# Rotation with copied halves, and other places for the tiles, in a hybrid attention block

## The chip, the cores and the metric

The kernel runs on one core of one Trainium2 chip. The metric is the time on the device of one run, in microseconds (us), as the median of several runs. A core has five engines with queues of their own: TensorE (PE; its weight loads are listed as PEld), VectorE (DVE), ScalarE (ACT), GpSimd (POOL) and SyncE (SP, which starts DMAs).

## What is computed

One decoder block for 512 tokens and width 2048. Its input is normalised and projected, two groups of heads attend in different ways, each head's output is gated by SiLU of a projection, and an output matrix and a second norm follow.

```
h = rmsnorm(x); proj = h @ w_in
qa, kca, vca, ksa, vsa, kwa, vwa, za, ga, qb, kb, vb, zb = split(proj)
qa, kca, ksa, kwa = rope(...)              # first group: 8 heads of 128, 2 key heads
kc, vc = compress(kca), compress(vca)      # blocks of 32 tokens, stride 16, small MLP
o_a = g0 * compressed_attention + g1 * selected_attention + g2 * window_attention
y_a = o_a * silu(za)
o_b = banded_attention(rope(qb), rope(kb), vb, window 128, sinks); y_b = o_b * silu(zb)
out = rmsnorm(x + concat(y_a, y_b) @ w_out)

def rope(x):  x1, x2 = halves(x); return concat(x1*cos - x2*sin, x2*cos + x1*sin)
```

## The kernel before

Every product of large matrices is made in fp32r words: an operand is kept as a high word (ACT rounds it into fp32r) and a low word (DVE subtracts the high word from the operand), and `mm3` (L118 to L121) issues three matmuls, high times high (L119), high times low (L120) and low times high (L121). So each weight tile that arrives in a `raw` buffer is split once by ACT into `whi` and once by DVE into `wlo`.

The stages, in the order of time: statistics and the first projections; from about 77 us the second head group (`softmax_b`, `attn_b`) with its projections, 512 columns wide; from 302 us the value projections (`tok_chunk`) and the compression (`compress_unit`); from 366 us the keys of the first group (`keys`, which calls `seven`, a product of 7 instead of 8 quarter products, as Strassen and Winograd do); from 423 us the eight heads of the first group (`pair`, which also calls `seven`, and `attn_a`); from 631 us the last head together with the first quarter of the output matrix; from 676 us the other quarters by the same seven products; from 789 us the end of the norm and the stores.

The order on each engine is not the order of the code: a scheduler with a model of its own for the time places the instructions, and `issue_after` pins a few.

**The rotation.** Channels lie on partitions, so the two halves of a head are partitions 0 to 63 and 64 to 127. `turn` (L658 to L666) makes two DVE products of 64 partitions, which read one half and the sine and write the other half of `t2` (L661), a product with the cosine (L662), and the sum (L664, on DVE for the keys and the last two heads, on POOL for the others). It runs four times for the keys and once for each head, twelve times in all. `turned` (L805 to L807) does the same for the keys to be compressed, from PSUM, twice, with `rope_mul` (L129 to L133). In `seven` the rotation of a finished row starts in the function `done`, behind the sum for the product "w"; the product "q" and the next row's products follow.

**Places.** Tiles lie at fixed addresses in each partition. In `words` (L82 and L83) the word tiles are 1088 elements wide and a unit of 1024 starts 0, 16, 32 or 48 elements in (MOVING, EVEN, STILL, BELOW), so that its start differs by 64 bytes. Small tiles named `space` move what is allocated behind them. `step` (L125 to L127) is one matmul into an unused bank, with a moving operand that starts at a chosen place.

## Time and profile before

| | us |
|---|---|
| median of 3 runs | 802.01 (801.76, 802.01 and 909.72) |
| the profiled execution | 802.8, of which its span is 801.0 |
| PE busy in the span | 789.6 |
| DVE busy | 686.3 |
| ACT busy | 504.7 |

Times in the rows are us from the start of the span, and a mean is in ns. Matmuls overlap in the pipeline: the listed length of one reaches from its start to its modelled end, and is longer than the step from one start to the next. TensorE's clock is granted in full (1.00, 2.4 GHz) in the stages from 302 to 789 us.

### The profile page before, as it was taken

To read this page: it belongs to the slowest core of one execution; us is meant where nothing else is said; L and a number is where in the kernel's file an instruction comes from. 1 tells how busy PE (TensorE), PEld (TensorE's weight loads), DVE (VectorE), ACT (ScalarE), POOL (GpSimd) and SP (SyncE) were. 2 spreads that over 40 slices of the span, in tenths; PEclk is the share of its full clock that TensorE was granted. 3 is DMA by queue.
4 is the path that set the end of the run, shared out by engine and by line. 5 is a ranking of instruction groups with operands and counts; after the bars stand their busy time and mean duration, and the time that the engine had idled before them with its cause. 6 is when DMAs were issued, how large, how long until landed. Compare 5 with 4: busy or idle time off the path is not lost.

```text
span 801.0 us, 15316 instructions
## 1 busy us (share of the span) xinstructions
PE 789.6 (99%) x5693; PEld 739.1 (92%) x5693; DVE 686.3 (86%) x1407; ACT 504.7 (63%) x1103; POOL 108.3 (14%) x111
## 2 busy tenths in 40 slices
PE   9999999999999999999999999999999999999996
PEld 8788888888888899999999999999999999999996
DVE  7668988889989597759999999998999798978895
ACT  6646657655666356664447778777777867553545
POOL 3615002110121000323210110110100000000000
PEclk9999999999999999999999999999999999999998
DMA  7572243564373469887723213225216836797845
GB/s 239 172 242 81 79 144 106 171 171 150 101 210 106 158 200 281 257 269 194 207 82 106 68 53 119 82 92 159 71 50 216 296 120 219 257 266 193 258 86 211
DMA packets 49563, 131.05 MB, mean 164 GB/s; under 512 B 6000, under 2 KB 8848, under 8 KB 49488
## 3 DMA queue, kind: packets, MB, share of 16 engines
q1 hardware_dynamic: 43376, 110.89, 42.3%
q0 software_dynamic: 5824, 18.65, 10.5%
q8 instruction: 45, 0.74, 0.4%
q10 hardware_dynamic: 288, 0.52, 0.2%
q14 instruction: 30, 0.25, 0.1%
HBM read 113.23 MB, written 16.81 MB: 162 GB/s over the span
## 4 chain that ended last, share of the span: by engine, by line
PE 86%; DVE 6%; DMA 3%; ACT 2%; issue 2%; POOL 0%; SPq 0%; DVEq 0%; ACTq 0%
PE pj L119 16%; PE pj L121 15%; PE pj L120 15%; PE oa L120 5%; PE oa L119 5%; PE oa L121 5%; PE sp L932 4%; PE bank L121 2%; PE bank L120 2%; PE bank L119 2%; DMA xr<-xT 2%; DVE wlo L543 2%; PE tp L969 2%; PE tp L384 2%; DMA raw<-wq 1%
## 5 line engine op out<-in xcount | busy, mean ns | idle before, releaser
L119 PE MATMUL pj<-xh,whi 128*128 128x256 f32 (+1 forms) x592 | 196.9, 333 | 0.6 <-ACT t L608 0.5
L121 PE MATMUL pj<-xh,wlo 128*128 128x256 f32 (+1 forms) x592 | 196.2, 331 | 0.0
L120 PE MATMUL pj<-xl,whi 128*128 128x256 f32 (+1 forms) x592 | 196.1, 331 | 0.0
L119 PEld LDWEIGHTS pj<-xh,whi 128*128 128x128 f32 x592 | 111.4, 188 | 11.0 <-ACT t L608 0.9
L121 PEld LDWEIGHTS pj<-xh,wlo 128*128 128x128 f32 x592 | 111.4, 188 | 10.1
L120 PEld LDWEIGHTS pj<-xl,whi 128*128 128x128 f32 x592 | 111.4, 188 | 9.7
L543 DVE TENSOR_TENSOR wlo<-raw,whi 128x1024 fp32r<-128x1024 f32 (+2 forms) x80 | 92.9, 1172 | 7.8 <-ACT whi L542 7.2
L542 ACT ACTIVATE whi<-raw 128x1024 fp32r<-128x1024 f32 (+2 forms) x80 | 77.6, 985 | 30.7 <-DVE raw L581 11.5
L99 DVE TENSOR_TENSOR wlo<-raw,whi 128x1024 fp32r<-128x1024 f32 (+1 forms) x61 | 72.1, 1184 | 22.8 <-ACT whi L97 22.3
L97 ACT ACTIVATE whi<-raw 128x1024 fp32r<-128x1024 f32 (+1 forms) x60 | 56.6, 945 | 28.8 <-PE pj L120 14.8
L120 PE MATMUL oa<-wlo,xh 128*128 128x256 f32 x200 | 55.5, 278 | 0.0
L119 PE MATMUL oa<-whi,xh 128*128 128x256 f32 x200 | 55.4, 278 | 0.0
L121 PE MATMUL oa<-whi,xl 128*128 128x256 f32 x200 | 55.2, 276 | 0.0
L121 PE MATMUL pj<-pu,wlo 128*128 128x256 f32 x160 | 45.0, 281 | 0.5 <-DVE wlo L543 0.5
L119 PE MATMUL pj<-pu,whi 128*128 128x256 f32 x160 | 45.1, 282 | 0.4 <-DVE zr L581 0.4
L120 PE MATMUL pj<-pu,whi 128*128 128x256 f32 x160 | 44.7, 279 | 0.0
L289 DVE TENSOR_TENSOR pl<-tp,ph 128x512 fp32r<-128x512 f32 (+1 forms) x64 | 40.7, 651 | 3.1 <-ACT ph L288 2.9
L288 ACT ACTIVATE ph<-tp 128x512 fp32r<-128x512 f32 (+1 forms) x64 | 34.1, 560 | 9.6 <-PE tp L969 4.4
L363 ACT ACTIVATE ttb<-ttb,sums 128x256 f32<-128x256 f32 (+1 forms) x64 | 30.0, 471 | 14.4 <-DVE sums L356 14.4
L121 PEld LDWEIGHTS oa<-whi,xl 128*128 128x128 f32 x200 | 37.6, 188 | 0.0
L120 PEld LDWEIGHTS oa<-wlo,xh 128*128 128x128 f32 x200 | 37.6, 188 | 0.0
L119 PEld LDWEIGHTS oa<-whi,xh 128*128 128x128 f32 x200 | 37.5, 188 | 0.0
(401 smaller groups left out, 2369.8 us busy)
## 6 DMA issues: line engine op xcount, KB each, us to landing
raw<-wq SPq DMA_DIRECT2D x41, 512.0 KB, 4.4
raw<-wz SPq DMA_DIRECT2D x36, 512.0 KB, 4.0
cw<-cw SPq DMA_DIRECT2D x32, 256.0 KB, 4.0
raw<-wos SPq DMA_DIRECT2D x14, 512.0 KB, 5.9
rw<-wos SPq DMA_DIRECT2D x10, 512.0 KB, 4.8
xr<-xT SPq DMA_DIRECT2D x16, 256.0 KB, 3.4
rows<-xT SPq DMA_DIRECT2D x8, 512.0 KB, 4.7
raw<-wo SPq DMA_DIRECT2D x8, 512.0 KB, 6.0
```

Of the source, the lines that this page charges most:

```text
L97: last["hi"] = act.activation(hi[:, :width], rw[:, :width], AF.Copy).ins
L99: last["lo"] = dve.tensor_tensor(out=lo[:, :width], in0=rw[:, :width], in1=hi[:, :width].bitcast(F32), op=ALU.subtract).ins
L119: pe.matmul(ps, ah, bh, start=first, stop=False, skip_group_check=go_on)
L120: pe.matmul(ps, ah, bl, start=False, stop=False, skip_group_check=go_on)
L121: recent["mm"] = pe.matmul(ps, al, bh, start=False, stop=last, skip_group_check=go_on).ins
L288: act.activation(ph, tp, AF.Copy)
L289: dve.tensor_tensor(out=pl, in0=tp, in1=ph.bitcast(F32), op=ALU.subtract)
L363: act.activation(tv, tv, AF.Exp, bias=mn[:, e, v:v + 1], scale=-1.0, accum_out=dn[:, e, v:v + 1])
L384: pe.transpose(tp[:, o:o + P], tts[kt + s][:, v, c0:c0 + P], ident)
L542: split_hi = act.activation(hi, src, AF.Copy).ins
L543: last["lo"] = dve.tensor_tensor(out=lo, in0=src, in1=hi.bitcast(F32), op=ALU.subtract).ins
L932: pe.matmul(sp[:, a:b], qq[:, qs], kk[:, ko:ko + b - a], start=pi == 0, stop=pi == 2)
```

## The change

**The rotation.** A new function, `swapped`, has ACT copy each half of the source onto the other half of `t2` (two copies of 64 partitions), and DVE multiply `t2` by the sine in place, all 128 partitions at once. The sine table is loaded with its halves exchanged, by two DMAs. `turn` and `turned` call it. Per rotation two DVE instructions become one, and ACT gets two.

**The places.** `gt` becomes the first tile and 64 bytes long (its last column goes to `small`, by a DMA of its own), `small`, `sums` and others grow or are moved, `vbf` shares the place of `ob`, `xh` and `xl` become two parts of one tile of 64 more elements, the constants for `words` change in six calls, and the low and high words of y are read back 16 elements further on. Nothing is computed in another way. What comes of it at the matmuls is this; the numbers are the start of the moving and of the stationary operand, in bytes within 256, as the two built programs have them:

| matmuls | before: moving, stationary | after |
|---|---|---|
| projections, 512 wide (L119 to L121) | 192, 192 | 192, 192 |
| second group: scores (L349, L350) | 192, 0 | 192, 0 |
| second group: transposes; output (L389, L390) | 128, 192 | 192, 0 |
| `tok_chunk` | 128, 192 | 128, 192 |
| `compress_unit` (L708, L709) | 64, 128 | 128, 192 |
| `seven`: all products | 192, 0 | 192, 0 |
| first group: scores (L932) | 192 or 64, 0 | 192 or 64, 0 |
| first group: transposes; output (L975 to L977) | 128, 192 | 192, 0 |
| output matrix, all quarters | 128, 192 | 192, 0 |

```diff
-MOVING, EVEN, STILL, BELOW = 0, 16, 32, 48
+MOVING, EVEN, STILL = 0, 16, 32
...
-    small = const.tile([P, 8], F32, name="small")
+    small = const.tile([P, 16], F32, name="small")
...
-    gt = const.tile([P, KT + 1], F32, name="gt")
-    rowvalid = gt[:, KT:KT + 1]
+    rowvalid = small[:, 8:9]
...
-    xh = xpool.tile([P, KT, S], F32R, name="xh")
-    xl = xpool.tile([P, KT, S], F32R, name="xl")
+    slabs = xpool.tile([P, 2 * KT * S + 64], F32R, name="x")
+    xh, xl = [slabs[:, e * KT * S:(e + 1) * KT * S].rearrange("p (k s) -> p k s", s=S) for e in range(2)]
...
-            nc.sync.dma_start(sinA, rope[:, 1, :])
+            for a, b in ((0, 64), (64, 0)):
+                nc.sync.dma_start(sinA[a:a + 64], rope[b:b + 64, 1, :])
...
+    def swapped(t2, v):
+        for a, b in ((0, 64), (64, 0)):
+            act.activation(t2[a:a + 64], v[b:b + 64], AF.Copy)
+        dve.tensor_tensor(out=t2, in0=t2, in1=sinA, op=ALU.mult)
+
     def turn(v, out=None, engine=None):
         t2 = wk.tile([P, S], F32, name="t2", tag="t2", bufs=1)
-        for a, b in ((0, 64), (64, 0)):
-            dve.tensor_tensor(out=t2[a:a + 64], in0=v[b:b + 64], in1=sinA[b:b + 64], op=ALU.mult)
+        swapped(t2, v)
         dve.tensor_tensor(out=v, in0=v, in1=cosA, op=ALU.mult)
...
-        t1, t2 = rope_mul(*[wk.tile([P, S], F32, name="t", tag=tag, bufs=1) for tag in tags], ps, cosA, sinA)
+        t1, t2 = [wk.tile([P, S], F32, name="t", tag=tag, bufs=1) for tag in tags]
+        swapped(t2, ps)
+        dve.tensor_tensor(out=t1, in0=ps, in1=cosA, op=ALU.mult)
...
-    places = [words(MOVING), words(BELOW), words(BELOW)]
+    places = [words(MOVING) for n in range(3)]
...
-    yh, yl = [[w[:, (2 * f + 1) % 17, :] for f in range(16)] for w in (xh, xl)]
+    yh, yl = [[slabs[:, (e * KT + (2 * f + 1) % 17) * S + 16:][:, 0:S] for f in range(16)] for e in range(2)]
...
-    step(banks1[3], flat[:, 3 * S - 16:3 * S + 112], flat[:, 2 * S + 32:2 * S + 288])
+    step(banks1[3], flat[:, 2 * S:2 * S + P], flat[:, 3 * S - 16:3 * S + 240])
...
-        hi, lo = to or words(MOVING)
+        hi, lo = to or words(EVEN)
```

The order on DVE at the keys of one head, the last stretch of `keys(1)`. `pj` is the bank of the product, `t` and `zr` the two rows to be rotated, and line numbers are those of each kernel. First the kernel before:

```order
L581 TENSOR_TENSOR t_3958<-t_3958,pj 128x256
L661 TENSOR_TENSOR t_4196<-t_3958,sinA 64x512 x2
L543 TENSOR_TENSOR wlo<-raw,whi 128x1024
L662 TENSOR_TENSOR t_3958<-t_3958,cosA 128x512
L581 TENSOR_TENSOR zr<-zr,pj 128x256
L543 TENSOR_TENSOR wlo<-raw,whi 128x1024
L664 TENSOR_TENSOR t_3958<-t_3958,t_4196 128x512
L661 TENSOR_TENSOR t_4293<-zr,sinA 64x512 x2
```

And DVE at the same place with the change:

```order
L584 TENSOR_TENSOR t_3962<-t_3962,pj 128x256
L546 TENSOR_TENSOR wlo<-raw,whi 128x1024
L664 TENSOR_TENSOR t_4200<-t_4200,sinA 128x512
L669 TENSOR_TENSOR t_3962<-t_3962,cosA 128x512
L584 TENSOR_TENSOR zr<-zr,pj 128x256
L671 TENSOR_TENSOR t_3962<-t_3962,t_4200 128x512
L546 TENSOR_TENSOR wlo<-raw,whi 128x1024
L773 TENSOR_TENSOR k_4207<-t_3962,k_4206 128x512
```

The sine product has moved behind one split of words (`wlo`) and is one instruction instead of two; the sum for `zr`, which frees a bank of PSUM, has four instructions between it and the sum for `t` in the first listing and three in the second.

ACT at that place, before (`whi` is the high word of a unit, `k` the rotated key):

```order
L753 ACTIVATE VC_2840<-vc 128x128
L542 ACTIVATE whi<-raw 128x1024 x2
L608 ACTIVATE t_4248<-pj 128x256
L542 ACTIVATE whi<-raw_4264 128x1024
L765 ACTIVATE k_4201<-t_3958 128x512
```

and with the change:

```order
L760 ACTIVATE VC_2841<-vc 128x128
L545 ACTIVATE whi<-raw 128x1024
L663 ACTIVATE t_4200<-t_3962 64x512 x2
L545 ACTIVATE whi<-raw 128x1024
L772 ACTIVATE k_4206<-t_3962 128x512
L663 ACTIVATE t_4299<-zr 64x512 x2
L611 ACTIVATE t_4254<-pj 128x256
```

The two copies stand between the two splits, so the second split now waits for the row `t_3962` and for the copies.

## Rows read from the trace of the kernel before

**Rows 1.** The page, part 1: busy us, share, instructions per engine.
```profile
PE 789.6 (99%) x5693; PEld 739.1 (92%) x5693; DVE 686.3 (86%) x1407; ACT 504.7 (63%) x1103; POOL 108.3 (14%) x111
```

**Rows 2.** Windows by stage: us, then busy us (instructions) per engine, clock, DMA.
```profile
302.00:366.00 64.00, 63.88 (x529) 63.66 (x528) 44.91 (x105) 39.31 (x96) 16.88 (x24) 1.00 0.87 260
366.00:423.00 57.00, 55.56 (x473) 54.60 (x474) 54.87 (x74) 27.65 (x40) 9.36 (x10) 1.00 0.54 152
423.00:631.00 208.00, 207.79 (x1746) 205.50 (x1746) 193.03 (x429) 160.55 (x401) 16.30 (x10) 1.00 0.36 117
631.00:676.00 45.00, 45.00 (x390) 44.73 (x389) 40.16 (x98) 34.88 (x84) 0.00 (x0) 1.00 0.53 183
676.00:789.00 113.00, 113.00 (x997) 112.86 (x997) 98.97 (x126) 58.18 (x84) 8.55 (x10) 1.00 0.72 205
```

**Rows 3.** Lines by shape, PE, 676 to 789 us: count, busy us, mean ns.
```profile
L120 PE MATMUL oa<-wlo,xh 128*128 128x256 f32 x144 | 39.7, 276 | 0.0
```

**Rows 4.** Windows of 5 us, PE alone: matmuls seen in each.
```profile
366.20:371.20 5.00, 5.00 (x44) 1.00 0.50 142
690.00:695.00 5.00, 5.00 (x46) 1.00 0.47 143
```

**Rows 5.** Lines by shape, PE, 423 to 631 us.
```profile
L120 PE MATMUL pj<-xl,whi 128*128 128x256 f32 x213 | 59.9, 281 | 0.0
...
L120 PE MATMUL pj<-pu,whi 128*128 128x256 f32 x104 | 29.1, 280 | 0.0
...
L120 PE MATMUL pj<-qw,whi 128*128 128x256 f32 x56 | 16.0, 285 | 0.0
...
L975 PE MATMUL op<-ph,VH 128*128 128x256 f32 x54 | 15.2, 282 | 0.0
```

**Rows 6.** Lines by shape, PE, 631 to 676 us.
```profile
L120 PE MATMUL oa<-wlo,xh 128*128 128x256 f32 x56 | 15.8, 282 | 0.0
...
L120 PE MATMUL pj<-wlo,xh 128*128 128x256 f32 x43 | 11.9, 278 | 0.0
```

**Rows 7.** Lines by shape, PE, 302 to 366 us.
```profile
L120 PE MATMUL bank<-wlo,xh 128*128 128x256 f32 x37 | 10.4, 281 | 0.0
...
L708 PE MATMUL bank<-whi,F 128*128 128x256 f32 x32 | 8.1, 280 | 0.0
```

**Rows 8.** Timeline, PE, around four transposes: start us, us, instruction.
```profile
450.59 0.36 PE L119 MATMUL pj<-xh,whi 128*128 128x256 f32 x1
450.79 0.28 PE L120 MATMUL pj<-xl,whi 128*128 128x256 f32 x1
```

**Rows 9.** Lines by shape, DVE, 366 to 423 us.
```profile
L543 DVE TENSOR_TENSOR wlo<-raw,whi 128x1024 fp32r<-128x1024 f32 x18 | 22.7, 1281 | 1.7 <-ACT whi L542 1.6
...
L661 DVE TENSOR_TENSOR t<-t,sinA 64x512 f32<-64x512 f32 x6 | 4.1, 686 | 0.1
...
L661 DVE TENSOR_TENSOR t<-zr,sinA 64x512 f32<-64x512 f32 x4 | 2.7, 686 | 0.1
...
L662 DVE TENSOR_TENSOR t<-t,cosA 128x512 f32<-128x512 f32 x3 | 2.1, 686 | 0.0
```

**Rows 10.** Waits of PE, 366 to 423 us: total us, times, longest us.
```profile
PE pj L121 <- DVE wlo L543: 0.5, 2, 0.3
PE pj L119 <- ACT t L608: 0.5, 1, 0.5
PE pj L119 <- DVE zr L581: 0.4, 1, 0.4
```

**Rows 11.** Timeline, DVE, the first rotation in this form: start us, us.
```profile
374.14 0.42 DVE L581 TENSOR_TENSOR t<-t,pj 128x256 f32<-128x256 f32 x1
...
374.60 1.39 DVE L661 TENSOR_TENSOR t<-t,sinA 64x512 f32<-64x512 f32 x2
...
377.76 0.41 DVE L581 TENSOR_TENSOR zr<-zr,pj 128x256 f32<-128x256 f32 x1
```

**Rows 12.** Chain of waits, 366 to 423 us, shares by line.
```profile
by line: DVE wlo L543 22.1%; DMA raw<-wq 13.1%; issue 12.1%; PE pj L119 10.7%; PE pj L121 10.7%; PE pj L120 10.0%; ACT whi L542 5.6%; DVE raw L581 4.0%; DVE t L661 3.8%; DVE t L581 3.2%; DVE zr L677 3.0%; DVE t L662 2.4%; DVE zr L581 2.3%; 
```

**Rows 13.** Lines by shape, ACT, whole span: a copy that changes partitions.
```profile
L395 ACT ACTIVATE ob<-opb 64x512 f32<-64x512 f32 x16 | 9.5, 594 | 14.0 <-PE opb L390 7.8 <-DVE ob L396 6.0
```

More of the change, by code (lines that the diff above doesn't have):

```diff
@@ L43, in hybrid_block @@
     const = ctx.enter_context(sb("const"))
+    gt = const.tile([P, KT], F32, name="gt")
     wp = ctx.enter_context(sb("wp", bufs=3))
@@ L121, in mm3 @@
         recent["mm"] = pe.matmul(ps, al, bh, start=False, stop=last, skip_group_check=go_on).ins
-    flat = xh.rearrange("p k s -> p (k s)")
+    flat = slabs[:, 0:KT * S]
     def step(bank, still, moving):
@@ L146, in load_x @@
         if k == 0:
-            nc.sync.dma_start(gt, gT)
+            nc.sync.dma_start(gt, gT[:, 0:KT])
         nc.sync.dma_start(xr, xT[:, k, :])
@@ L202, in hybrid_block @@
         nc.sync.dma_start(tab, tabs)
+        nc.sync.dma_start(rowvalid, gT[:, KT:KT + 1])
     dve.tensor_tensor(out=cosB, in0=cosB, in1=rstdb, op=ALU.mult)
@@ L290, in split_pt @@
         return ph, pl
-    vbf = wb.tile([P, NQ, P], F32, name="vbf")
+    vbf = wb.tile([P, NQ, P], F32, name="vbf", tag="ob")
+    KBH = wb.tile([P, 2, S], F32R, name="KBH")
+    KBL = wb.tile([P, 2, S], F32R, name="KBL")
     sk = wb.tile([P, 5, 16], F32, name="sk")
@@ L295, in hybrid_block @@
     act.activation(sk[:, 1, :], sk[:, 0, :], AF.Copy, scale=-1.0)
-    KBH = wb.tile([P, 2, S], F32R, name="KBH")
-    KBL = wb.tile([P, 2, S], F32R, name="KBL")
     VB = wb.tile([P, NQ, 2, P], F32R, name="VB")
@@ L338, in softmax_b @@
         for part in range(2):
-            sums = wk.tile([P, 3, 2, 2], F32, name="sums", tag="sums")
+            sums = wk.tile([P, 6, 2, 2], F32, name="sums", tag="sums")
             mn, dn, ex = sums[:, 0], sums[:, 1], sums[:, 2]
@@ L497, in hybrid_block @@
     VC = [kv.tile([P, P], F32R, name=f"VC{g}") for g in range(2)]
+    kv.tile([P, 48], F32, name="space")
     ahead = ExitStack()
@@ L855, in hybrid_block @@
             cacc[1] = bank(4)
-        compress_unit(1, u, cacc[1], words(BELOW))
+        compress_unit(1, u, cacc[1], words(MOVING))
         if 1 <= u <= 3:
@@ L887, in hybrid_block @@
     KH, KL = [kv.tile([P, CMP + 1056], F32R, name=f"K{e}")[:, 0:CMP + 1024] for e in "HL"]
+    kv.tile([P, 16], F32, name="space")
     for e, k in enumerate((KH, KL)):
@@ L915, in attn_a @@
             tt = wa.tile([P, 1792 if pair else 768], F32, name=f"tt{pair}", tag=f"tt{pair}")
-            sums = wk.tile([P, 2, 2, 3], F32, name="sums", tag="sums")
+            sums = wk.tile([P, 4, 2, 3], F32, name="sums", tag="sums")
             mn, dn = sums[:, 0], sums[:, 1]
@@ L1152, in hybrid_block @@
                      (1, 3, (7,))):
-        hi, lo = load_unit(wo0[:, c, u], 1024, place=MOVING, loaded=first_units.pop(0) if first_units else None, after=last["qh"],
+        hi, lo = load_unit(wo0[:, c, u], 1024, place=EVEN, loaded=first_units.pop(0) if first_units else None, after=last["qh"],
                            after_lo=low_y[11] if (c, u) == (0, 2) else last["turn"])
@@ L1166, in hybrid_block @@
                 combos(m)
+    cmb.tile([P, 48], F32, name="space3")
     banks1 = banks(1)
-    step(banks1[3], flat[:, 3 * S - 16:3 * S + 112], flat[:, 2 * S + 32:2 * S + 288])
+    step(banks1[3], flat[:, 2 * S:2 * S + P], flat[:, 3 * S - 16:3 * S + 240])
     for T in range(2):
@@ L1336, in pair @@
             def pair():
-                return words(MOVING)
+                return words(EVEN)
             def hi(d, src):
```

## Prediction

> **What bounds the kernel now.** I read the page's first part, then the windows by stage, then lines, waits and the chain stage by stage. The first part shows TensorE (PE) busy for 789.6 of 801.0 us and VectorE (DVE) for 686.3 [rows 1]. So what does not shorten PE's own work or its waits changes nothing. The windows then show two kinds of stage [rows 2]. In the heads (423 to 631 us) PE is busy 207.79 of 208.00 us, and at the output matrix (676 to 789) all the time: here only a matmul's own pace counts. At the keys (366 to 423) DVE is busy 54.87 of 57.00 us and PE issues only 473 matmuls, while at the output matrix 997 take 113.00 us, 113.3 ns each. By that pace the keys need 473 x 113.3 ns = 53.6 us of PE. The other 3.4 us of the stage are waits and slower matmuls, and the chain of waits says on whom: the splits into low words on DVE hold 22.1%, the sine products (L661) 3.8% more [rows 12].
>
> The second thing to see is that equal matmuls have two paces. A 128x256 product lists 276 ns at the output matrix [rows 3] and 280 to 285 ns in the heads [rows 5], without a wait ahead of either. That it is a real difference and not one of the listing shows in two windows of 5 us: 46 matmuls against 44 [rows 4], at the same clock (1.00). The change can act on both: the rotation on DVE's load, the places on the pace.
>
> **The change, part by part.**
>
> *Rotation, on DVE.* Twelve calls of `turn` and two of `turned` each lose two products of 64 partitions and get one of 128. A product with 64 partitions costs 686 ns and one with 128 also 686 [rows 9], so each rotation saves DVE 0.69 us, 9.6 us in all. Only those at the keys can matter: ten of the L661 instructions (6 + 4) lie there, five rotations, so DVE's 54.87 us fall by 5 x 0.69 = 3.4 to 51.4 us, under PE's 53.6. How much of it PE gets: its three waits at this stage for DVE or ACT add up to 0.5 + 0.5 + 0.4 = 1.4 us [rows 10]. One can be followed in the order shown: the sum for `zr`, which frees the bank for which PE waits 0.4 us, starts 3.62 us after the sum for `t` (377.76 less 374.14) [rows 11], and with one sine product less in between it starts about 0.69 us earlier. Below, the gain is bounded by nothing (13.1% of the chain there is loads of `wq`, which stay [rows 12]), above by the 3.4 us. I take 1.7: the waits, and a little of the pace that is lost behind them, nearer to the waits since these are seen.
>
> *Rotation, on ACT.* 28 copies are added. The nearest row is a copy of 64 partitions by 512 from PSUM to others, 594 ns [rows 13]; the copies in `turned` are of this kind, those in `turn` read SBUF, so this row is an estimate for them. At the keys ACT gets 10 x 0.594 = 5.9 us on 27.65 of 57; in the heads seven rotations add 14 x 0.594 = 8.3 us on 160.55 of 208 [rows 2]. Both have room, and I cost them at nothing. What hides them at the keys is the split of 1.28 us (L543) [rows 9] that now stands on DVE between the sum and the sine product: two copies take 1.19. Without that cover a rotation is longer than before by 2 x 0.594 + 0.686 - 2 x 0.686 = 0.50 us, and behind the copies wait the next high word and, for it, DVE's low word and PE's product.
>
> *The sine table and `rowvalid`.* Two DMAs instead of one, and one small one more on SP's queue behind the tables at the end of the first stage. Their first readers are far behind them; nothing.
>
> *Places, first group's heads.* Before, products (moving start 192, stationary 0) alternate with transposes and outputs (128, 192); afterwards all are (192, 0), but for parts of the scores. The nearest rows of a stretch where products, transposes and outputs agree are those of the last head with the first quarter of the output matrix, all (128, 192). Count what each stretch has over 276 ns, with the middle line (L120) of each triplet standing for its three. Heads: 3 x (213 x 5 + 104 x 4 + 56 x 9 + 54 x 6) ns = 6.9 us over 1281 matmuls, 5.4 ns each [rows 5]. Last head: 3 x (56 x 6 + 43 x 2) ns = 1.3 us over 297, 4.3 ns each [rows 6]. If the heads come to the same, they gain 1.1 ns x 1281 = 1.4 us, which I take. Bounds: at most 6.9, less what stays because the first product behind transposes is long (360 ns against 280 for the next) [rows 8]; and a loss, if moving starts that jump by 64 bytes were what brings the fast pace back, since then the change takes such jumps away. At worst all 1281 run at 5 ns over, with the long ones on top, about 1 us more than now.
>
> *Places, values and compression (302 to 366 us).* `tok_chunk` and `compress_unit` alternate between (128, 192) and (64, 128), and both become (128, 192). The products list 281 ns and the compression's 280 [rows 7]. At 276 they would gain 3 x 37 x 5 ns and 2 x 32 x 4 ns, 0.8 us together. I take half, 0.4, and nothing as the lower end.
>
> *Places, output matrix.* From (128, 192) to (192, 0), in itself uniform before and after, and at 276 ns before [rows 3]. I take no change.
>
> *A rule against it.* The row shows 46 against 44 matmuls in equal times [rows 4], on stretches whose operands lie at different places but also follow different work. The Trainium skill, "TensorE: Matmul & The Clock Gate", Part 2 (Step-by-step), says that PE has two independent SBUF read ports and that loading the next weights takes no read bandwidth from the running matmul. By that rule a place could not set the pace, and the sum would be the rotation's 1.7 us alone. No row here separates the place from what ran just before, so the rule stands as the first rival.
>
> **Sum.** 1.7 (keys) + 1.4 (heads) + 0.4 (values) = 3.5 us from the profiled execution's 802.8 us (span 801.0 and 1.8 around it): 799.3. That execution is 0.8 us over the median of the runs, 802.0, from which the same sum gives 798.5. I forecast 799.0.
>
> **Rivals.**
>
> 1. *The places do nothing.* The pace comes from the work before, whatever the starts. For it: within one stretch of equal places the lines still read 276 to 285. Only the rotation is left: 802.8 - 1.7 = 801.1 us.
> 2. *The fast pace everywhere.* For it: uniform places go together with 276 ns for 997 matmuls [rows 2, 3]. Against it: the scores still change places, and in the last head uniform places did not suffice [rows 6]. Keys 3.4, values 0.8, and of the heads' 6.9 some 5.5, since the long first products stay: 802.8 - 9.7 = 793.1 us.
> 3. *The output matrix falls into the slow pace.* (192, 0) there is new, and the one `step` that sets it is new too. If those 997 matmuls run 5 ns longer (281 against 276), that is 5.0 us; with the keys' gain and none in the heads 802.8 + 5.0 - 1.7 = 806.1 us, slower. It decides as soon as over 35% of that stage is slow, for then it takes back the 1.7. Against it: a uniform stretch has held the fast pace for 113 us.
> 4. *The copies become the wait.* ACT works in order, and ACT's own waits in front of a copy hold the splits behind it. At 0.50 us for each of the five rotations at the keys that is 2.5 us of PE, with no gain there: 802.8 + 2.5 - 1.8 (heads, values) = 803.5 us. It decides where ACT comes to the copies later than DVE is through its split. ACT's 27.65 busy us of 57 speak against it.
>
> **How the numbers follow.** Forecast (796 to 801, its own range) 0.45; rival 1 (801 to 802) 0.19; rival 2 0.11; rival 3 0.11; rival 4 0.11; something else, beyond 2% either way, 0.03. A range from 793.0 to 805.0 leaves out rival 3, that rest, and about half of rival 2's spread, just under 2 in 10. A change of 2%, 16 us, is about what a measurement of this kernel can tell from no change. None of the cases reaches it: all bounds together are 3.4 + 6.9 + 0.8 = 11.1 us of gain. So faster 0.01, within 2% 0.97, slower 0.02.
>
> **What would show it.** Right: DVE's busy time between the values and the heads falls by about 3.4 us and that stage shrinks by 1 to 2 us; PE's wait for `zr` is gone; outputs of the heads (`op`) list under 282 ns; 997 matmuls of the output matrix still in 113 us. Wrong: DVE's sine product shows idle time in front of it that ends with ACT's copy (rival 4); the lines of the output matrix list 281 (rival 3); the heads' lines are as before and only the stage of the keys is shorter (rival 1). What would break the whole forecast is the scheduler's new interleaving in the heads: a PE that waits there (0.21 us of idle now) would cost more than any term of this sum.

## The result: 0.9% slower, lost in the heads

The changed kernel takes **810.8 us** (809.1 to 811.6 in four runs) against 802.7 of the kernel before beside it: a ratio of **1.0093, 95% interval 1.0076 to 1.0111**. (The ratio is of the fast runs alone, while the median 802.7 still counts a run of 909.7 us, so it is not the quotient of the two medians.) The forecast was 799.0 us with a range to 805.0; it missed, on the slow side. The class of within 2% is right, the sign is not. The profiled execution of the changed kernel took 810.6 us, of which its span is 808.7.

The page's first part, busy us by engine (for the kernel before: [rows 1]):

```profile
PE 794.2 (98%) x5693; PEld 741.5 (92%) x5693; DVE 681.5 (84%) x1393; ACT 523.7 (65%) x1131; POOL 109.1 (13%) x111
```

DVE is busy 4.8 us less, half of the 9.6 that the prediction worked out, and ACT 19.0 us more. The span is 7.7 us longer, of which PE is busy for 4.6.

To compare stage by stage, the borders have to follow the products: a stage goes from its first product to the first one of the next. In the kernel before these are at 291.1 (values, compression and keys), 420.6 (heads), 620.6 (last head with most of the first quarter of the output matrix) and 664.0 (the end of that quarter and, from 678.8, the other three; "output matrix" below). The windows of [rows 2] have the values 11, the heads 2 and the last head 10 us later than this; no term of the sum hangs on it. Windows by stage, the kernel before: us, then busy us (instructions) of PE, its weight loads, DVE, ACT and POOL, clock, DMA.

```profile
291.10:420.60 129.50, 128.46 (x1082) 127.51 (x1081) 107.96 (x204) 71.93 (x149) 26.24 (x34) 1.00 0.73 215
420.60:620.50 199.90, 199.17 (x1668) 196.64 (x1667) 189.25 (x410) 154.39 (x384) 16.30 (x10) 1.00 0.32 101
620.50:664.00 43.50, 43.50 (x376) 43.23 (x374) 36.17 (x90) 31.27 (x73) 0.00 (x0) 1.00 0.56 200
664.00:793.20 129.20, 129.20 (x1140) 129.06 (x1139) 111.12 (x160) 72.52 (x120) 8.55 (x10) 1.00 0.73 218
```

The same four stages of the changed kernel:

```profile
290.80:421.20 130.40, 128.90 (x1084) 127.70 (x1083) 105.32 (x206) 79.07 (x161) 27.49 (x34) 1.00 0.72 215
421.20:626.20 205.00, 202.15 (x1677) 197.74 (x1676) 186.58 (x402) 164.92 (x400) 15.21 (x10) 1.00 0.30 96
626.20:669.60 43.40, 42.65 (x360) 42.06 (x359) 36.43 (x90) 30.47 (x71) 0.00 (x0) 1.00 0.61 216
669.60:801.00 131.40, 131.36 (x1148) 131.17 (x1146) 112.28 (x162) 72.38 (x120) 8.55 (x10) 1.00 0.72 214
```

Of the 7.8 us between the two profiled executions the heads hold 5.0, the output matrix 2.1 and values and keys 1.0. Eight transposes of the last head stand in the heads now, so about 0.9 us of the 5.0 is work that has only moved. In the heads PE now idles 2.85 us where it idled 0.7. What it waits for there (changed kernel, PE, 421 to 626 us; total us, times, longest):

```profile
PE pj L121 <- DVE wlo L546: 0.9, 3, 0.6
PE op L986 <- DVE pl L290: 0.8, 2, 0.7
PE sp L942 <- DVE sums L948: 0.5, 1, 0.5
PE sp L942 <- POOL ql L262: 0.3, 1, 0.3
PE pj L119 <- ACT t L611: 0.3, 1, 0.3
```

There is no single culprit: low words, the low words of the probabilities (`pl`), the low word of the queries (`ql`). What stands behind them is on DVE's list of waits in the same stretch:

```profile
DVE wlo L546 <- ACT whi L545: 5.2, 11, 0.9
...
DVE t L664 <- ACT t L663: 1.4, 4, 0.5
```

DVE, the busy engine of that stage, stands 11 times for ACT's high words and 4 times for ACT's copies (L663). In the kernel before it stands twice for high words there:

```profile
DVE wlo L543 <- ACT whi L542: 0.5, 2, 0.3
```

**One rotation followed.** The row is `t`; its last sum, the sine product, the cosine product, the sum on POOL, the high word `qh` (ACT) and the low word `ql` (POOL) follow each other. The kernel before, timeline of DVE around the second head (start us, us):

```profile
437.38 0.42 DVE L581 TENSOR_TENSOR t<-t,pj 128x256 f32<-128x256 f32 x1
437.83 1.39 DVE L661 TENSOR_TENSOR t<-t,sinA 64x512 f32<-64x512 f32 x2
...
440.39 0.69 DVE L662 TENSOR_TENSOR t<-t,cosA 128x512 f32<-128x512 f32 x1
```

its ACT, with the high word:

```profile
442.58 0.64 ACT L260 ACTIVATE qh<-t 128x512 fp32r<-128x512 f32 x1 [0.94 <-POOL t L664]
```

and its POOL:

```profile
441.24 1.30 POOL L664 TENSOR_TENSOR t<-t,t 128x512 f32<-128x512 f32 x1 [21.12 <-DVE sums L950]
443.29 2.31 POOL L261 TENSOR_TENSOR ql<-t,qh 128x512 fp32r<-128x512 f32 x1 [0.75 <-ACT qh L260]
```

The row is ready at 437.80, the sum starts 3.4 us later, `qh` ends 5.4 us behind the row, and `ql` ends at 445.60. The changed kernel at the same place, DVE:

```profile
437.78 0.42 DVE L584 TENSOR_TENSOR t<-t,pj 128x256 f32<-128x256 f32 x1
...
441.24 0.69 DVE L664 TENSOR_TENSOR t<-t,sinA 128x512 f32<-128x512 f32 x1 [0.37 <-ACT t L663]
441.85 0.69 DVE L669 TENSOR_TENSOR t<-t,cosA 128x512 f32<-128x512 f32 x1
```

its ACT:

```profile
438.40 0.71 ACT L958 ACTIVATE tt<-tt,sums 128x512 f32<-128x512 f32 x1
...
439.11 0.71 ACT L958 ACTIVATE tt<-tt,sums 128x512 f32<-128x512 f32 x1
...
439.93 1.27 ACT L663 ACTIVATE t<-t 64x512 f32<-64x512 f32 x2
...
443.20 0.70 ACT L967 ACTIVATE pc<-tc__4758,sums 128x128 f32<-128x128 f32 x2
443.79 2.35 ACT L969 ACTIVATE tt<-tt,sums 128x384 f32<-128x384 f32 x4
446.03 0.63 ACT L688 ACTIVATE st<-zr 128x512 f32<-128x512 f32 x1
446.55 0.63 ACT L261 ACTIVATE qh<-t 128x512 fp32r<-128x512 f32 x1
```

and its POOL:

```profile
442.70 1.58 POOL L671 TENSOR_TENSOR t<-t,t 128x512 f32<-128x512 f32 x1 [22.35 <-DVE t L669]
447.25 1.57 POOL L262 TENSOR_TENSOR ql<-t,qh 128x512 fp32r<-128x512 f32 x1 [2.96 <-ACT qh L261]
```

The row is ready at 438.20, but ACT is in its two exponentials (L958) and begins the copies 1.7 us later. The sum starts 4.5 us behind the row instead of 3.4. Then `qh` stands on ACT behind the weights' products (L967, L969) and a tanh (L688), which the scheduler has put ahead of it, and ends 9.0 us behind the row instead of 5.4. `ql` ends at 448.82, and the score product that needs it waits.

How much room was there? Slack is the time from the end of a query word to the start of the first score product that reads it, from the trace, for the eight heads in turn (us):

| kernel | slack of `qh` | slack of `ql` |
|---|---|---|
| before | 2.0 2.2 1.2 2.1 2.0 1.9 2.0 1.7 | 0.7 1.3 **0.2** 1.9 1.6 **0.4** 2.1 1.6 |
| changed | 2.4 0.9 1.5 2.5 1.8 2.2 2.5 1.0 | 1.3 **0.1 0.1** 1.2 0.3 1.0 2.1 **0.2** |

A slack of 0.1 (0.05 in the trace) means that PE took the word as soon as it was there. The kernel before had as little as 0.2 us in hand for the low words of two heads.

### The profile page after: what moved, and what is told of

It is laid out like the page before. It is cut to its first block, busy times and chain, and to the rows that moved or that the text cites. A ratio compares the mean times of both kernels' runs of the same rounds, so it can differ in the third digit from the quotient of the medians.

```text
span 808.7 us, 15340 instructions
## 1 busy us (share of the span) xinstructions
PE 794.2 (98%) x5693; PEld 741.5 (92%) x5693; DVE 681.5 (84%) x1393; ACT 523.7 (65%) x1131; POOL 109.1 (13%) x111
## 4 chain that ended last, share of the span: by engine, by line
PE 43%; DVE 6%; ACT 2%; issue 1%; DVEq 0%; ACTq 0%
PE pj L121 7%; PE pj L120 7%; PE pj L119 7%; PE oa L120 5%; PE oa L121 5%; PE oa L119 5%; PE sp L942 3%; DVE wlo L546 2%; DVE raw L584 2%; PE tp L979 1%; PE op L986 1%; PE op L987 1%; PE op L985 1%; ACT whi L545 1%; PE op L1002 1%
## 5 line engine op out<-in xcount | busy, mean ns | idle before, releaser
L119 PE MATMUL pj<-x,whi 128*128 128x256 f32 (+1 forms) x592 | 197.3, 333 | 0.5 <-ACT t L611 0.3
L121 PE MATMUL pj<-x,wlo 128*128 128x256 f32 (+1 forms) x592 | 196.8, 333 | 0.9 <-DVE wlo L546 0.8
L120 PE MATMUL pj<-x,whi 128*128 128x256 f32 (+1 forms) x592 | 195.8, 331 | 0.0
L121 PEld LDWEIGHTS pj<-x,wlo 128*128 128x128 f32 x592 | 111.5, 188 | 11.9 <-DVE wlo L546 1.7
L119 PEld LDWEIGHTS pj<-x,whi 128*128 128x128 f32 x592 | 111.3, 188 | 11.6 <-ACT t L611 0.9
L120 PEld LDWEIGHTS pj<-x,whi 128*128 128x128 f32 x592 | 111.3, 188 | 9.7
L120 PE MATMUL oa<-wlo,x 128*128 128x256 f32 x200 | 55.7, 279 | 0.0
L121 PE MATMUL oa<-whi,x 128*128 128x256 f32 x200 | 55.6, 278 | 0.0
L119 PE MATMUL oa<-whi,x 128*128 128x256 f32 x200 | 55.4, 278 | 0.0
L121 PE MATMUL pj<-pu,wlo 128*128 128x256 f32 x160 | 45.2, 283 | 0.8 <-DVE wlo L546 0.8
L119 PE MATMUL pj<-pu,whi 128*128 128x256 f32 x160 | 45.5, 284 | 0.0
L120 PEld LDWEIGHTS oa<-wlo,x 128*128 128x128 f32 x200 | 37.6, 188 | 0.2 <-DVE wlo L1354 0.2
L584 DVE TENSOR_TENSOR raw<-raw 128x1024 f32<-128x1024 f32 x28 | 37.4, 1337 | 0.3
L119 PEld LDWEIGHTS oa<-whi,x 128*128 128x128 f32 x200 | 37.6, 188 | 0.0
```

The costliest lines, as they stand in the source:

```text
L119: pe.matmul(ps, ah, bh, start=first, stop=False, skip_group_check=go_on)
L120: pe.matmul(ps, ah, bl, start=False, stop=False, skip_group_check=go_on)
L121: recent["mm"] = pe.matmul(ps, al, bh, start=False, stop=last, skip_group_check=go_on).ins
L584: return dve.tensor_tensor(out=out, in0=a, in1=b, op=op).ins
```

## The experiments

Theory A says that the copies in the heads cost the time, theory B that the places do, theory C that any change gives the scheduler an interleaving that may be worse. The table has all runs. The stages go from first product to first product, in the one execution of each kernel that was profiled: for rot_alone the slowest of its four, for products_new_order the fastest. The heads of changed, rot_alone, heads_rot and products_new_order hold the eight transposes more (0.9 us), those of after_pool_copies 27 matmuls more (3.1 us). "Idle" is what PE's steps in the heads, from one matmul's start to the next, are longer than the plain step of their shape, where that is over 130 ns. Ratios are to the kernel before, run on the same chip.

| run | median us | ratio (95%) | values and keys | heads | idle | last head | output |
|---|---|---|---|---|---|---|---|
| before | 802.7 | | 129.5 | 200.0 | 0.7 | 43.4 | 129.2 |
| changed | 810.8 | 1.0093 (1.0076 to 1.0111) | 130.5 | 205.0 | 4.9 | 43.5 | 131.3 |
| rot_alone | 809.2 | 1.0083 (1.0057 to 1.0108) | 129.8 | 207.3 | 5.5 | 43.1 | 131.7 |
| places_alone | 804.5 | 1.0013 (1.0001 to 1.0026) | 128.4 | 200.3 | 1.0 | 44.3 | 129.2 |
| keys_rot | 803.4 | 1.0010 (0.9994 to 1.0026) | 128.9 | 199.6 | 0.2 | 44.3 | 129.7 |
| heads_rot | 809.1 | 1.0076 (1.0059 to 1.0094) | 128.6 | 205.4 | 4.9 | 43.6 | 130.6 |
| copies_old_order | 809.2 | 1.0070 (1.0055 to 1.0085) | 128.8 | 204.3 | 4.4 | 44.6 | 130.3 |
| products_new_order | 812.0 | 1.0108 (1.0092 to 1.0125) | 128.0 | 207.6 | 6.7 | 43.4 | 130.6 |
| sum_on_dve | 808.6 | 1.0065 (1.0046 to 1.0084) | 128.7 | 205.2 | 4.3 | 43.1 | 130.5 |
| dve_sum_old_order | 809.2 | 1.0075 (1.0060 to 1.0090) | 128.7 | 204.9 | 4.7 | 44.5 | 129.2 |
| idle_copies | 805.3 | 1.0022 (1.0010 to 1.0035) | 129.1 | 200.3 | 1.3 | 44.3 | 129.2 |
| pool_copies_old_order | 802.8 | 0.9999 (0.9989 to 1.0009) | 128.4 | 199.7 | 1.1 | 44.1 | 129.2 |
| after_pool_copies | 814.6 | 1.0149 (1.0107 to 1.0191) | 131.5 | 212.8 | 7.6 | 40.3 | 129.8 |
| first_quarter_128 | 809.1 | 1.0078 (1.0063 to 1.0093) | 129.0 | 199.6 | 0.2 | 44.5 | 134.1 |
| two_steps | 805.2 | 1.0017 (1.0007 to 1.0028) | 129.7 | 200.3 | 1.0 | 44.5 | 130.0 |
| before_steps_keys | 803.3 | 1.0011 (0.9985 to 1.0037) | 130.8 | 200.2 | 0.7 | 43.4 | 129.3 |

**1. Which part, and where.** Four kernels take the change apart: the rotation alone on the old places, the places alone, and on the new places the rotation at the keys alone or in the heads alone. Since the sine table now has its halves exchanged, a product by DVE comes out with the other sign, and the difference is taken instead of the sum. The edit of keys_rot (heads_rot has it at the keys and in `turned`):

```diff
+        if copied:
+            swapped(t2, v)
+        else:
+            for a, b in ((0, 64), (64, 0)):
+                dve.tensor_tensor(out=t2[a:a + 64], in0=v[b:b + 64], in1=sinA[b:b + 64], op=ALU.mult)
...
+        op = ALU.add if copied else ALU.subtract
...
-            turn(qv, engine=pool if h < 6 else dve)
+            turn(qv, engine=pool if h < 6 else dve, copied=False)
```

> The kernel before with the rotation alone (copies on ACT, sine table with exchanged halves), all tiles at the old places. Theory A (the copies lengthen the rotation in the heads and hold up ACT's high words, so that PE waits there: PE's idle time in the heads of the changed kernel is 4.9 us in 12 gaps over 130 ns, 0.7 in one before): the heads take about 205 us from the first score product to the first product of the output matrix against 200.0 before, the output matrix stays at 129.2, the total about 807 to 808. Theory B (the places cost it): heads as before, total 801 to 803. Theory C (any change of durations gives the scheduler another interleaving, some with waits): heads anywhere from 200 to 205, with PE's gaps at other places than in the changed kernel.

> The changed kernel with the old rotation (two half products on DVE, sine table as before), all tiles at the new places. Theory A: heads at 199 to 200 us (their slow-paced matmuls 3.2 instead of 3.8 us over), output matrix at 130 to 131.3 against 129.2 because 274 of its matmuls fall into the slow pace there, total 802.5 to 804. Theory B: heads 204 to 205, output matrix 131, total 808 to 810. Theory C: heads anywhere from 199 to 205.

> The changed kernel, but the rotations of the eight heads on DVE again (two half products, their difference taken instead of the sum since the sine table has its halves exchanged); copies remain at the keys. Theory A: the gaps of the heads go, total 804 to 805 (810.8 less 5, plus what the copies at the keys do). If the copies at the keys hurt by themselves, the stretch of values and keys stays at about 130.5 us against 129.5 before. Theory B: still about 810. Theory C: heads anywhere from 199 to 205.

> The changed kernel, but the rotations of the keys on DVE again; copies remain in the eight heads. Theory A: heads at about 205 us with gaps of 4 to 5 us in all, total 809 to 811. Theory B: about 810 as well, so this run tells A from B only together with the other three. Theory C: heads anywhere from 199 to 205.

It is the copied rotation in the heads: the three kernels that have it (rot_alone, heads_rot, changed) take 205.0 to 207.3 us there, the three that don't 199.6 to 200.3. Theory A holds for the heads. For the output matrix it does not: it expected a loss there from the places (130 to 131.3 us), but places_alone has 129.2 and rot_alone, on the old places, 131.7. The places alone cost 1.0 us by the medians (interval 0.1 to 2.1); the last head is 0.9 us longer, values and keys 1.1 shorter in the profiled execution. The copies at the keys neither help nor hurt in the total. One thing made the next step possible: places_alone has the order of the kernel before instruction by instruction on every engine, and rot_alone that of the changed kernel, so the rotation alone decides the order. It is the rotation in the heads: keys_rot has the heads in the order of places_alone, heads_rot in that of the changed kernel.

**2. The copies or the order.** Two kernels exchange the order: the copied rotation in the order of places_alone, and the products in the order of heads_rot. `QUEUES` holds the names of the instructions of PE, DVE, ACT and SP in the wanted order, from the first head on; an edge sets the order of issue on its engine and adds no wait.

```diff
+    traced = {i.name: i for i in nc.cur_bb.bb.instructions}
+    for row in QUEUES:  
...
+        for a, b in zip(names, names[1:]):
+            tc.add_manual_dep(traced[b], a, mybir.DependencyInfo(mybir.DependencyClass.NoSync,
+                              mybir.DependencyReason.DATA), reason="queue")
```

> The kernel of the run heads_rot (copied rotation in the eight heads, new places), with every other instruction of PE, DVE, ACT and SP from the first head on held in the order that places_alone has; only the two copies and the sine product of each rotation stand where the scheduler puts them. If the order alone makes the loss (what ran longer is nothing by itself), the heads come to 200 to 200.5 us as in places_alone and the total to 803.5 to 805. If the copies themselves do (ACT's 1.2 us for each rotation, the rotation's longer way to the queries' words), the heads stay near 205 and the total at 808 to 809. In between, the share tells how much belongs to each.

> The kernel of the run places_alone (two sine products on DVE), with every instruction of PE, DVE, ACT and SP from the first head on held in the order of heads_rot; the two products stand in place of its one. If the order alone makes the loss, the heads come to about 205 us and the total to 808.5 to 809.5, with PE's gaps at the same instructions as in heads_rot. If the copies do, heads about 200 and the total 803.5 to 805.

Neither alternative holds alone. The copies cost 4.0 us in the old order (204.3 against 200.3), and the new order costs 7.3 us without any copy (207.6), of which 0.9 are the moved transposes. In the new order the copies are the cheaper form (205.4 in heads_rot). DVE of products_new_order, in the heads:

```profile
DVE wlo L545 <- ACT whi L544: 5.3, 11, 0.9
```

These are the eleven waits for high words of the changed kernel (5.2 us), without a copy: they belong to the order. In copies_old_order the waits are plain to read. DVE, in the heads:

```profile
DVE t L664 <- ACT t L663: 9.4, 5, 2.9
DVE wlo L546 <- ACT whi L545: 3.0, 6, 0.9
```

and PE, in the same stretch:

```profile
PE op L989 <- DVE pl L290: 1.4, 1, 1.4
PE sp L945 <- POOL ql L262: 0.6, 1, 0.6
PE sp L945 <- ACT qh L261: 0.6, 1, 0.6
```

The largest, followed back. ACT of copies_old_order:

```profile
592.11 2.35 ACT L972 ACTIVATE tt<-tt,sums 128x384 f32<-128x384 f32 x4
594.48 1.27 ACT L663 ACTIVATE t<-t 64x512 f32<-64x512 f32 x2
```

and DVE:

```profile
590.79 0.41 DVE L584 TENSOR_TENSOR t<-t,pj 128x256 f32<-128x256 f32 x1
...
595.78 0.69 DVE L664 TENSOR_TENSOR t<-t,sinA 128x512 f32<-128x512 f32 x1 [2.87 <-ACT t L663]
...
602.13 1.28 DVE L290 TENSOR_TENSOR pl<-tp,ph 128x512 fp32r<-128x512 f32 x2
```

and PE:

```profile
602.87 0.39 PE L989 MATMUL op<-pl,VH 128*128 128x256 f32 x1 [1.40 <-DVE pl L290]
```

The row is ready at 591.2. ACT has four products, 2.35 us in all, ahead of the copies, which start 3.3 us behind the row; DVE stands 2.87 us before its sine product, all that is behind it on DVE is late, and at 602.87 PE waits 1.40 us for `pl`. That both queues are served strictly in order is also what the Trainium skill says ("PSUM — Partial Sum Buffer", Engine vs sequencer instructions, of ScalarE's and VectorE's queues); this trace agrees.

**3. What about the copies.** The way from the row to the query words may be too long, ACT may be too loaded, or DVE may stand behind ACT's queue. The sum on DVE shortens the way (once with the scheduler free, once in the old order):

```diff
-            turn(qv, engine=pool if h < 6 else dve)
+            turn(qv)
```

> The kernel of the run heads_rot with the sum of the rotation on DVE in all heads instead of POOL in the first six, and the scheduler free. The rotation's way from the row to the queries gets about 0.9 us shorter (1.58 us on POOL against 0.69 on DVE), about the 1.06 us by which the copies made it longer. If the length of that way decides which interleaving the scheduler makes, the heads come back to 200 to 201 us and the total to 803.5 to 805. If any change gives an arbitrary interleaving, anything from 200 to 205 may come.

> The kernel of sum_on_dve (copies on ACT, sum of the rotation on DVE in all heads), held in the order of places_alone. Slack is the time from the end of a query word (qh, ql) to the score product that needs it; in places_alone it is 1.1 to 2.2 us for qh and 0.2 to 2.1 us for ql, in copies_old_order it is used up (0.05 us) for three of the sixteen words and PE waits 3.5 us more. Theory D (the lateness of the query words is what costs): the way is 0.6 to 0.9 us shorter in the first six heads, the slack comes back in part, the heads take 202 to 203 us (204.3 in copies_old_order, 200.3 in places_alone), total 805.5 to 807.5. Theory E (DVE stands behind ACT's copies, 9.4 us in five waits, and all that is behind it on DVE is late): the sum makes no difference there, heads 204 to 205, total 808.5 to 810.

It gains nothing: 205.2 and 204.9. DVE's wait for the copies is the same 9.4 us in five times as in copies_old_order. Theory D falls, E holds. Then the load without the wait, in the order of copies_old_order:

```diff
         for a, b in ((0, 64), (64, 0)):
+            if spare is not None:
+                act.activation(spare[a:a + 64], rstdb[b:b + 64, 0:384], AF.Copy)
+        for a, b in ((0, 64), (64, 0)):
             dve.tensor_tensor(out=t2[a:a + 64], in0=v[b:b + 64], in1=sinA[b:b + 64], op=ALU.mult)
```

> Two sine products on DVE in the heads as in places_alone, and on ACT, at the very places in the queue where copies_old_order has its copies, two copies of 64 partitions by 384 of a constant, whose result nobody reads; every other instruction stands as in copies_old_order. So ACT's extra load stays (about four fifths of it), and only DVE's wait for the copies is gone. If the lateness of the copies costs (DVE stands behind ACT's queue), the heads come to 200 to 201 us and the total to 803.5 to 805. If ACT's load costs (its high words and exponentials come later), the heads stay at 203.5 to 204.3 and the total at 807.5 to 809.

The heads are back at 200.3 with ACT busy for 161.2 us there (154.7 in places_alone). So ACT does have the room; the prediction was right in that, and it did not help. (Here the copies wait for no row; in copies_old_order ACT stands 0.4 us in all in front of its copies, so that difference is small.) And the wait without ACT, copies by POOL:

```diff
-            act.activation(t2[a:a + 64], v[b:b + 64], AF.Copy)
+            pool.tensor_copy(t2[a:a + 64], v[b:b + 64])
```

> The kernel of heads_rot with the two copies of each head's rotation on POOL instead of ACT (POOL is busy 16 of 208 us in the heads), held in the order of places_alone. POOL has nothing in its queue when a row is ready, so the copies start at once; ACT's load is that of the kernel before. If it is the queue on ACT that makes the copies late (in copies_old_order they start up to 3.3 us after the row), the heads come to 200.5 to 202.5 us and the total to 804 to 806. If any rotation that is longer than two DVE products costs as much, or if POOL's copies take as long as the wait on ACT, the heads stay at 204 or above and the total at 808 or more.

Lines of POOL by shape in the heads of this run (count, busy us, mean ns, idle time before them):

```profile
L663 POOL COPY t<-t 64x512 f32<-64x512 f32 x14 | 12.3, 878 | 149.1 <-DVE t L584 84.4 <-ACT whi L545 39.5 <-DVE sums L964 24.9
```

The mean hides two lengths. All copies of the run, with the shortest, the median and the longest in ns:

```profile
L663 POOL COPY t<-t x16: 607/612/1652, 412.5 to 613.3; 64x512 f32<-64x512 f32 x16
```

In the heads ten of the fourteen take 0.61 us, about ACT's 0.63, and four take 1.5 to 1.65, each beside one of DVE's splits (`wlo`); two copies that follow each other take up to 2.3 us, against 1.27 on ACT. Yet the heads take 199.7 us, as without the change, because POOL has nothing ahead of it: DVE waits for copies 2.3 us in all here, 9.4 with ACT. A free engine, some of whose copies are slower, beat one with a queue. Copies on ACT that stand ahead of the four products, and not behind them, were not tried.

**4. The same repair with the scheduler free.** The changed kernel with the heads' copies on POOL:

> The changed kernel with one difference: the copies of the eight heads' rotations are made by POOL; those at the keys stay on ACT, and the scheduler is free. If ACT's queue was the whole cause, the heads come to 199.5 to 201 us (205.0 in the changed kernel), the total to 803 to 805, as in pool_copies_old_order with its held order. If the scheduler's own interleaving costs as well, the heads stay at 202 or more and the total at 806 or more.

The heads take 212.8 us. PE waits 2.9 us in five times for `pl`; it also waits 2.8 us for the first `qh`, ahead of the heads' first product. So the interleaving that the scheduler makes costs by itself, with the same copies in the heads: 9.3 us against the held order over heads and last head together (253.0 against 243.8), which leaves out what only moved between the two. Why its model prefers such an order was not tried.

**5. The pace.** In the last head places_alone has 303 matmuls at the slow pace, the kernel before 99, in the same order of instructions: 1.39 against 0.48 us over the plain steps. One constant of places_alone puts the first quarter's words back to a start of 128:

```diff
-        hi, lo = load_unit(wo0[:, c, u], 1024, place=EVEN, loaded=...
+        hi, lo = load_unit(wo0[:, c, u], 1024, place=MOVING, loaded=...
```

> The kernel of places_alone with one constant changed: the words of the first quarter of the output matrix start where they do in the kernel before (moving start 128 instead of 192); order and all else are the same. In places_alone 303 of the 309 counted matmuls of the stretch of the last head run at the slow pace (1.39 us over), in the kernel before 99 of 308 (0.48 us). If a jump of the moving start from 128 to 192 brings the fast pace back, the slow ones fall to about 100 to 150 and the stretch from 44.28 to 43.3 to 43.7 us, total 0.6 to 0.9 us below places_alone (803.6 to 803.9). If the pace comes from the work before alone, 44.2 to 44.4 us as now.

The last head comes out as the second alternative had it, 44.5 us, but neither foresaw what follows: the output matrix takes 134.1 us instead of 129.2. Only its first 15 us belong to the first quarter; the three quarters behind it have the instructions, places and order of places_alone. Lines by shape, PE, 690 to 790 us, first_quarter_128:

```profile
L120 PE MATMUL oa<-wlo,x 128*128 128x256 f32 x123 | 34.5, 281 | 0.0
```

In [rows 3] that line lists 276. One matmul more in front of them,

```diff
-    step(banks1[3], flat[:, 2 * S:2 * S + P], flat[:, 3 * S - 16:3 * S + 240])
+    for at in (3 * S, 3 * S - 16):
+        step(banks1[3], flat[:, 2 * S:2 * S + P], flat[:, at:at + 256])
```

> The kernel of first_quarter_128 with one matmul more: the matmul into an unused bank ahead of the second quarter (moving start 128) now follows one at 192, so that the moving start goes 128, 192, 128, 192 instead of 128, 128, 192. In first_quarter_128 all of the output matrix behind it ran at the slow pace (134.1 us against 129.2 in places_alone, where the start goes 192, 128, 192). If the jump is what sets the pace, that stage comes back to 129.2 to 129.5 and the total to 803.5 to 805. If the first quarter's words at 128 keep it slow by something else, 134 and 808.5 to 810.

and the stage is back at 130.0 us; the 0.8 over 129.2 are slow matmuls ahead of that one (0.7) and the matmul itself (0.1). The same line of two_steps:

```profile
L120 PE MATMUL oa<-wlo,x 128*128 128x256 f32 x128 | 35.3, 276 | 0.0
```

So the pace is a state, which lasted for the 134 us of this stage. The added matmul starts at 192, so that the one behind it jumps to 128 and the next product back to 192; with that jump the pace was fast. The other profiles agree: all of them but first_quarter_128 have a jump at that matmul, and in five (changed, rot_alone, heads_rot, products_new_order, sum_on_dve) the products ahead of it were slow and those behind it fast. Lines by shape of the changed kernel, PE, 669.7 to 685.7 us and 686.5 to 779 us:

```profile
L120 PE MATMUL oa<-wlo,x 128*128 128x256 f32 x29 | 8.1, 281 | 0.0
...
L120 PE MATMUL oa<-wlo,x 128*128 128x256 f32 x128 | 35.3, 276 | 0.0
```

At the keys this was tried in the kernel before (the same ahead of the products p and u):

```diff
+        if i < 2:
+            step(pb[:, H0], xh[:, 2, 0:P], flat[:, 3 * S - 16:3 * S + 240])
         prod(pb[:, H0], u0, "22", True)
```

> The kernel before with six matmuls more: at the keys, ahead of the products 22, p and u of both key heads, one matmul with moving start 128 into the region that the product then overwrites; all else and the order as before. Each costs 0.12 us, 0.7 in all. If such a matmul brings the fast pace back, the slow matmuls of the keys fall from 533 to 300 or fewer (2.8 us over to 1.5), and the total comes 0.5 us below before at best, so a ratio of 0.9990 to 1.0000. If it does nothing there, the total is 0.7 us above before.

That is inconclusive: 500 slow matmuls instead of 533, and an interval that holds both expectations. Nor is such a matmul a sure cure: of the six added, one (at 358.2 us) has products at the fast pace behind products at the slow one, one (354.9) leaves them slow, and one right behind a wait (381.1) has 47 slow products behind it.

No version beats the kernel before: the best, pool_copies_old_order, equals it.

## Why the prediction was wrong, step by step

- **Rotation, on ACT: cost nothing.** This is the step that failed. "Both have room" was read from busy shares (160.55 of 208 us), and idle_copies shows the room is there. But a copy needs ACT at one moment, and what counts is what stands ahead of it in the queue then: 1.7 us in the changed kernel's second head, 3.3 us at 591 in copies_old_order. The prediction worked out that a rotation without cover gets 0.50 us longer, at the keys only, and put the heads at nothing without naming a cover. There the sum starts 1.06 us later behind the row in the rotation shown, and the low words of two heads had 0.2 and 0.4 us of slack. The measured price of the copies is 4.0 us in the old order.
- **The scheduler's new interleaving.** The prediction named it as what "would break the whole forecast", at the right place, and then gave it no price and a share of the 0.03 for the rest. It should have been a rival: products_new_order puts 7.3 us on it (6.4 without the moved transposes), the changed kernel's heads came out 5.0 longer. How much of those 5.0 is order and how much late copies can't be split: the two don't add.
- **Rival 4** (the copies become the wait) had the mechanism, at the wrong stage: it was priced for five rotations at the keys, where DVE has a split as cover, and not for the heads, which have seven more.
- **Rotation, on DVE: -1.7 at the keys.** DVE's busy time fell by 2.6 us (107.96 to 105.32; 3.4 were said) and PE's wait for `zr` is gone, as said. The stage did not get shorter: other waits for low words took its place, and 269 of the products of 256 columns at the keys ran at the slow pace instead of 137 (0.6 us). PE at values and keys of the changed kernel:

```profile
PE pj L121 <- DVE wlo L546: 1.1, 3, 0.5
PE pj L119 <- DVE t L584: 0.2, 1, 0.2
```

  Nor could one profile have shown 1.7 us: places_alone, first_quarter_128 and two_steps have the same values and keys and take 128.4, 129.0 and 129.7 us there.
- **Places, heads: -1.4.** Nothing came of it: with the order and the rotation of the kernel before the heads take 200.3 us in places_alone and 199.6 in first_quarter_128, against 200.0. The loss of the lower bound, "if moving starts that jump by 64 bytes were what brings the fast pace back", showed in the last head, 44.3 against 43.4 us. That stretch [rows 6] was taken for one of uniform places, but its scores start at 192 or 64 and all else at 128, so it had jumps too.
- **Places, values: -0.4.** It came, and a little more: from the first of these products to the first at the keys 62.4 us before and 61.7 in places_alone. Of 314 products of 256 columns 211 were slow before, 55 in places_alone and 52 in the changed kernel. Lines by shape, PE, 291 to 353 us, the kernel before and places_alone:

```profile
L121 PE MATMUL bank<-whi,xl 128*128 128x256 f32 x62 | 17.3, 280 | 0.0
...
L121 PE MATMUL bank<-whi,x 128*128 128x256 f32 x62 | 17.1, 276 | 0.0
```

  In the changed kernel the stretch takes 62.5 us all the same: it holds four products that stood ahead of it (0.45 us) and a wait (0.4). And sum_on_dve, on the same places, had 241 slow: the places favour a pace here, they don't fix it.
- **Output matrix: 0.** Right for the places (129.2 us in places_alone). The changed kernel has 2.1 us more there: seven matmuls that came over from the last head (0.8 us), 274 products at the slow pace instead of 10 (1.2), a longer wait (0.1). As rot_alone has 131.7 us there on the old places, this came with the rotation. Rival 3's price of 5.0 us is what first_quarter_128 shows for the whole stage, 4.9; in the changed kernel a quarter of it happened.
- **The evidence for two paces** [rows 4] was misread, by the prediction and by its rule against it. The window at the keys has 44 matmuls instead of 46 not because its products are slower: from 366.74 to 370.37 us they start every 113 to 114 ns. What it lacks went into four short matmuls (L749) and steps of 0.2 us around them. The kernel before, timeline of PE:

```profile
367.08 0.28 PE L119 MATMUL pj<-pu,whi 128*128 128x256 f32 x1
367.19 0.28 PE L120 MATMUL pj<-pu,whi 128*128 128x256 f32 x1
...
370.48 0.38 PE L749 MATMUL bank<-cw2s,sr 128*128 128x128 f32 x2
```

  The two paces are real (experiment 5); this row does not show them. Nor is 2% what a measurement of this kernel can tell: the interval of the result is 0.35% wide.
- **Rival 1 and the rule behind it.** The rows gave it 0.19. The Trainium skill, "TensorE: Matmul & The Clock Gate", Part 2 (Step-by-step), says that PE has two independent SBUF read ports, one for the streaming operand and one for the loading of weights. That a start place then changes nothing is what the prediction drew from it; the section does not speak of start places. One constant changed 129.2 to 134.1 us and one matmul changed it back to 130.0 at the same clock, so here the measurement decides: places act, through a state, and not as a property of the place in use.

## What to carry to other kernels

Before work is moved to an engine "with room", read on its timeline what stands ahead in its queue when the input is ready, and measure the slack of the result at its reader; a busy share answers neither. Where a scheduler sets the order, a changed instruction can buy a new order (the copies in the heads did, those at the keys left the heads as they were), and that order needs a price of its own: hold the old order, run both, and only then judge the change. An idle engine can be the better place even if some of its copies are slower.

## What was not expected of the hardware

- Two paces of the same matmul at full clock, 113.3 ns from start to start (129.20 us by 1140) and 117.6 (134.10 by 1140), are a state that outlasts a thousand matmuls; one matmul more, and with it a jump of the moving start, brought the fast pace back (134.1 against 130.0 us for the stage). Which sequences set it to slow stays open, and the same places and order can come out at either pace.
- A copy of 64 partitions by 512 takes ACT 632 ns from SBUF and 592 from PSUM. POOL takes 0.61 us alone and 1.5 to 1.65 beside a split of DVE (pool_copies_old_order; in after_pool_copies 0.61, and 1.46 to 1.58).
